# A two-layer decoder trunk on one core: one quarter's output product made plain, weight combinations made in other stages, operand sums in small steps, the last attention block by block

## The chip, the cores and the metric

The kernel runs on one core of one Trainium2 chip, in one launch. The metric is device time in microseconds; of several runs the median counts. Engines are named as the profile names them: PE multiplies matrices (PEld is its loading of weights), DVE, ACT and POOL work on vectors, SP issues nearly all transfers, in the order of its queue.

## What is computed

Sequence 2048, width 1024, float32. A first layer (A) gates with mixed values, a second (B) attends in three groups of 8 query heads over one shared set of keys and values.

```
# layer A
h = rms_norm(x, norm_g) * (1 + scale) + shift
u, v, z = jnp.split(h @ w_in, 3, axis=-1)          # each 2048 wide
v = rms_norm(jax.nn.gelu(v), sgu_g)
mixed = jnp.einsum('gts,bcsge->bctge', w_causal, v) + b_s
y = gelu(u) * mixed * jax.nn.silu(z)
x = x + gate * (y @ w_out)                         # the output product
# layer B: k, v from x @ w_kv (6 heads of 128, three groups)
qz = h @ w_in                                      # 24 query heads of 128, and z
o_g = banded attention of group g (128 keys back, dilation 1, 4, 16)
o = softmax over groups of their log-sums, times o_g, summed
x = x + gate * ((o * silu(z)) @ w_out)
```

## The kernel before

**Products.** Each float32 operand is held as a high part and a low part. A product of a 128-wide strip is three matmuls of 128x512 (`mm3`, L282): high by high, high by low, low by high. Weights come as 256 KB loads `raw_*` and `split` (L253) makes the two parts: ACT copies the high part, DVE subtracts to get the low one. Some products are Strassen–Winograd products of 2x2 blocks, with 7 block products in place of 8 and sums of operands, weights and results around them.

**Stages.** The 2048 tokens are four quarters of 512, numbered Q = 0 to 3 here; the "quarter 2" of the change's name is Q = 1. Layer A runs in halves H = 0 and 1. `layer_in(H)` (L1127) makes v (H = 0 with `plain_v`, H = 1 with `dense_v` for the weight blocks 4 and 5), then u and z in `gate_block`s with the mixing. `layer_out(Q)` (L1215) is the output product, then `proj_B(Q)` (L1332) makes layer B's projections: `kv_block(2)`, `kv_block(1)`, `q_block(2)`, `kv_block(0)`, `q_block(1)`, `q_block(0)`, `z_block`. The order is H = 0, Q = 0, Q = 1, H = 1, Q = 2, Q = 3. `finish()` is the last stage: the weighted sum of the three attentions and layer B's output product (`pf`).

**Output product.** For Q = 0 it is plain (`dense`, 384 matmuls). For Q = 1 to 3 it is `dense_o` (L445, 7 products, 336 matmuls). Its weights are the seven combinations 11, 21, 22, t1 to t4 of w_out, which `combine_out` (L387) makes once: for each h (2) and k (4) it loads w_out into `co` tiles, keeps the split parts as `cs` tiles and stores them to `wtd`; four subtractions run on POOL (L415). `o_weights` (L439) loads them back in 512 KB pieces.

**Side work.** Work beside the main products stands in generators, the fillers. `tick()` in the main loops steps them; `rate` says how many steps a tick gives. What a step writes lands in the engines' and SP's queues between the main work's instructions, and those queues run in order. The fillers that the change moves are `combine_out` (beside Q = 0's output product, rate 3.0), `more_side_work` (`combine_weights((4, 5))`: the v weights' combinations of H = 1, POOL subtractions `cw` at L340 to L343 and stores to `wt`; and `presplit`: layer B's w_out split and stored to `wod`; beside Q = 1's output product, rate 1.0), and attention of earlier quarters (`attend_local`, `wide_attention`). `sums_h` makes the sums of h that are operands of the Strassen products, at once where it is called. Scheduling by the framework can shift instructions within an engine's queue, so the order of the queues is shown where it matters.

## Time and profile before

| | |
|---|---|
| median of 3 runs (lowest, highest) | 3053.54 us (3048.94, 3057.72) |
| profiled execution | 3048.26 us, its span 3046.2 us |
| PE busy, share of span | 2878.5 us, 94% |
| PEld | 2385.4 us, 78% |
| DVE, ACT, POOL | 71%, 55%, 24% |
| mean granted clock of PE | 0.98 |
| transfers | 765.92 MB, 251 GB/s |

Stages in the profiled execution, by their first and last matmuls: first v product to 242 us; u and z of H = 0 to 592; output of Q = 0 592 to 715 and its projections to 950; output of Q = 1 950 to 1053, projections to 1323; v of H = 1 1323 to 1489; u and z 1489 to 1962; output of Q = 2 1962 to 2052; projections to 2274; output of Q = 3 2274 to 2387; projections to 2724; the last stage to 3041. Matmuls are pipelined, so a busy PE can still be waiting inside a busy interval: the distance from one matmul to the next is a better measure than busy time.

### The profile page before, as it was taken

What the parts mean: (1) busy time and instruction counts of PE and PEld (TensorE: products, weight loads), DVE (VectorE), ACT (ScalarE), POOL (GpSimd) and SP (SyncE); (2) the same over time, 40 slices, a digit from 0 to 9 for tenths busy, and PEclk for the clock granted to TensorE, in tenths of its full rate; (3) what the DMA queues carried; (4) which work ended last, traced back from release to release, by engine and by line L of the source; (5) the groups of instructions that cost most, each with busy time, mean ns of one, the idle gap of its engine ahead of it and who ended that gap; (6) DMA issues with size and microseconds to landing.
All of it is one profiled execution on the core that took longest, in us unless ns stands there. A gap on an engine that the chain in (4) does not pass through costs nothing. (4 is left out here: it accounts for less than half of the span.)

```text
span 3046.2 us, 44925 instructions
## 1 busy us (share of the span) xinstructions
PE 2878.5 (94%) x14338; PEld 2385.4 (78%) x14338; DVE 2159.3 (71%) x4033; ACT 1670.3 (55%) x3411; POOL 735.1 (24%) x975
## 2 busy tenths in 40 slices
PE   8899999978999898989999999999999999999999
PEld 5678888866787676768888888878888778878897
DVE  5777778667785565774557887957776867879782
ACT  4544444435564345765676676636554558865551
POOL 1102540032432232500001242401423321122212
PEclk9999999989999999999999999999999999999999
DMA  8898997578889979785445445697789667796643
GB/s 301 281 316 287 318 320 253 204 291 296 276 261 348 378 261 317 258 293 169 153 150 170 157 147 159 229 378 225 253 298 325 204 222 248 256 337 228 205 164 121
DMA packets 390080, 765.92 MB, mean 251 GB/s; under 512 B 43242, under 2 KB 99788, under 8 KB 387924
## 3 DMA queue, kind: packets, MB, share of 16 engines
q1 hardware_dynamic: 389844, 763.06, 73.3%
q8 instruction: 113, 1.85, 0.3%
q14 instruction: 123, 1.01, 0.1%
HBM read 552.53 MB, written 210.38 MB: 250 GB/s over the span
## 5 line engine op out<-in xcount | busy, mean ns | idle before, releaser
L284 PE MATMUL pd_kv<-w_kv,hkh 128*128 128x512 f32 x672 | 215.4, 400 | 13.0 <-DVE w_kv L256 9.0
L284 PE MATMUL pd_v<-w_v,opa 128*128 128x512 f32 x672 | 164.8, 402 | 12.7 <-ACT w_v L255 10.0
L284 PEld LDWEIGHTS pd_kv<-w_kv,hkh 128*128 128x128 f32 x672 | 127.7, 192 | 43.7 <-DVE w_kv L256 12.6
L284 PEld LDWEIGHTS pd_v<-w_v,opa 128*128 128x128 f32 x672 | 126.6, 192 | 43.4 <-ACT w_v L255 10.1
L284 PE MATMUL pd_kv<-w_kv,hkl 128*128 128x512 f32 x336 | 132.8, 396 | 0.0
L255 ACT ACTIVATE w_q<-raw_q 128x512 fp32r<-128x512 f32 x144 | 88.3, 627 | 62.2 <-DMA raw_q<-in_b_w_in_dram 30.1
L1555 ACT ACTIVATE pr<-pr,stat,rt 128x256 f32<-128x256 f32 (+1 forms) x192 | 104.1, 544 | 28.6 <-DVE stat L1549 24.2
L256 DVE TENSOR_TENSOR w_q<-raw_q,w_q 128x512 fp32r<-128x512 f32 x144 | 99.0, 707 | 28.6 <-ACT w_q L255 28.2
L1381 POOL TENSOR_SCALAR s_q<-s_q 128x4 f32<-128x4 f32 x96 | 24.0, 250 | 356.9 <-DVE s_q L1380 287.3
L1806 PE MATMUL pf<-wo,yb 128*128 128x512 f32 x256 | 106.0, 414 | 0.1
L1563 POOL TENSOR_TENSOR dg<-pr,ident 128x256 f32<-128x256 f32 x30 | 25.6, 854 | 321.8 <-ACT pr L1555 297.2
L284 PE MATMUL pd_o<-w_o,yh 128*128 128x512 f32 x256 | 85.4, 414 | 17.1 <-ACT w_o L255 14.6
L1808 PE MATMUL pf<-wo,yb 128*128 128x512 f32 x256 | 100.9, 394 | 0.5 <-DVE yb L1767 0.5
L1807 PE MATMUL pf<-wo,yb 128*128 128x512 f32 x256 | 100.5, 392 | 0.0
L1555 ACT ACTIVATE st_pr<-st_pr,stat,rt 128x256 f32<-128x256 f32 (+1 forms) x128 | 73.4, 575 | 31.2 <-DVE stat L1549 19.2
L1163 POOL TENSOR_SCALAR rvs<-rvs 128x8 f32<-128x8 f32 x2 | 0.8, 416 | 353.0 <-DVE rvs L1162 353.0
L1615 PEld LDWEIGHTS po<-kvr,pT 128*128 128x128 f32 x640 | 78.3, 191 | 9.8 <-ACT pT L1455 4.5
L1615 PE MATMUL po<-kvr,pT 128*128 128x128 f32 x640 | 81.6, 276 | 3.9 <-ACT pT L1455 2.4
L1814 POOL TENSOR_TENSOR of<-of,xr 128x512 f32<-128x512 f32 x32 | 41.4, 1293 | 176.2 <-DVE of L1813 153.3
L1180 ACT ACTIVATE vc<-vc,rvs 128x256 f32<-128x256 f32 x128 | 54.7, 498 | 53.2 <-DMA vc<-vd 42.8
L1545 DVE SCALAR_TENSOR_TENSOR pr<-dist,rt,ps 128x256 f32<-128x256 f32 (+1 forms) x192 | 70.8, 416 | 17.2 <-PE ps L1542 13.6
L340 POOL TENSOR_TENSOR cw<-cw 128x512 f32<-128x512 f32 x24 | 35.0, 1457 | 190.3 <-DMA cw<-in_a_w_in_dram 103.9
(1885 smaller groups left out, 8918.9 us busy)
## 6 DMA issues: line engine op xcount, KB each, us to landing
raw_q<-in_b_w_in_dram SPq DMA_DIRECT2D x144, 256.0 KB, 3.7
w_o<-wtd SPq DMA_DIRECT2D x72, 512.0 KB, 7.4
wtd<-cs SPq DMA_DIRECT2D x56, 512.0 KB, 3.5
qt<-qd SPq DMA_DIRECT2D x96, 260.0 KB, 3.2
wt<-cw SPq DMA_DIRECT2D x96, 256.0 KB, 4.2
od<-ot SPq DMA_DIRECT2D x96, 256.0 KB, 5.6
raw_kv<-in_w_kv_dram SPq DMA_DIRECT2D x84, 256.0 KB, 4.2
raw_v<-in_a_w_in_dram SPq DMA_DIRECT2D x80, 256.0 KB, 4.4
```

The source lines that it names most:

```text
L255: nc.scalar.activation(hi, src, AF.Copy)
L256: nc.vector.tensor_tensor(lo, src, hi.bitcast(F32), ALU.subtract)
L284: last_mm[0] = nc.tensor.matmul(pt, a, u[:, w, :], start=f, stop=e, skip_group_check=more)
L340: e.tensor_tensor(t1, t3, t1, ALU.subtract)
L1180: nc.scalar.activation(v[:, c, :], v[:, c, :], AF.Copy, scale=rvs[:, i:i + 1])
L1545: nc.vector.scalar_tensor_tensor(pr[:, i, :], dist[:, 256 - w:256], u["rt"][:, h:h + 1], psc[:, i, :], ALU.mult, ALU.add)
L1555: nc.scalar.activation(pr[:, i, :], pr[:, i, :], AF.Exp, bias=mneg[:, i:i + 1], scale=u["rt"][:, h:h + 1], accum_out=lsum[:, i:i + 1])
L1615: nc.tensor.matmul(po[:, h * P:(h + 1) * P], u["pT"][h // hp][:, h % hp, j, :], u["kv"][:, j, kh, 1, :], start=j == 0, stop=j == nk - 1)
L1806: nc.tensor.matmul(pt, yb[:, 0, k, :], w_[:, 0, :], start=k == 0, stop=False)
L1807: nc.tensor.matmul(pt, yb[:, 0, k, :], w_[:, 1, :], start=False, stop=False)
L1808: nc.tensor.matmul(pt, yb[:, 1, k, :], w_[:, 0, :], start=False, stop=k == KT - 1)
L1814: nc.gpsimd.tensor_tensor(o_, o_, xr, ALU.add)
```

## The change

- The output product of Q = 1 becomes plain: `fast = Q >= 2`.
- `combine_out` keeps only t1 to t4, its 32 subtractions run on DVE, and it stands beside Q = 1's projections (rates 2.4 and 0.8). The weights 11, 21 and 22 of Q = 2 and 3 are loaded raw and split each time.
- `more_side_work` stands beside Q = 0's projections (rates 2.6 and 1.1). The output products of Q = 0 and 1 have no side work (rate 0).
- `sums_h` is a filler whose steps load one k ahead; for H = 1 the sums are completed between products of `dense_v`.
- The gates of H = 1 run with rate 1.55 (1.7 before) and Q = 2's output with 2.0 (1.5).
- The last attention (`attend_local(3, ...)`): its group g = 1 starts beside Q = 3's z block, the local group follows block by block, each block weighed as it is done; no bursts, rate 6 (8).

```
-    wtd = dp.tile([2, 7, 4, P, 2, 512], F32, name="wtd")
+    wtd = dp.tile([2, 4, 4, P, 2, 512], F32, name="wtd")
...
-                yield from keep((4, t1), (5, t4))
-                yield from keep((6, t2))
                 for o, a, b in ((t1, t3, t1), (t3, t2, t3), (t2, t2, t1), (t4, t4, t2)):
-                    nc.gpsimd.tensor_tensor(o, a, b, ALU.subtract)
-                yield
+                    nc.vector.tensor_tensor(o, a, b, ALU.subtract)
...
     def o_weights(Q, w, h):
+        if w[0] != "t":
+            return wunits(a_w_out, 8 * h + 4 * (w[0] == "2"), 512 * (w[1] == "2"), f"o{Q}{w}{h}_", 4)
...
             for j in range(4):
-                if j == 2:
+                if j == 1:
                     ops.update({n: op_tile(f"a0{n}") for n in ("s1", "s2")})
-                    for _ in sums_h(0, ops, False):
-                        pass
+                    sa = sums_h(0, ops, False)
+                    fillers.append(sa)
+                    rate[0] = 2.2
                 plain_v(1, j, b)
+            complete(sa)
...
                 dense_v(1, b, ops, lambda t, n, src, dst, junk, b=b: v_put(1, t, 2 * (b - 4) + n, src, dst, junk),
-                        {} if b == 5 else {"11": lambda: sums(False, "s2", "s1"),
-                                           "21": lambda: sums(True, "s4", "s3", "22")})
+                        {} if b == 5 else {"11": lambda: complete(sa), "21": second,
+                                           "t1": lambda: complete(sb[0])})
...
-        rate[0] = 0.65 if H == 0 else 1.7
+        rate[0] = 0.65 if H == 0 else 1.55
...
-        fast = Q >= 1
+        fast = Q >= 2
...
-        rate[0] = 1.7 if Q < 3 else 3.4
+        if Q == 0:
+            fillers.append(more_side_work())
+        if Q == 1:
+            co.append(combine_out())
+            fillers.append(co[0])
+        rate[0] = (2.6, 2.4, 1.7, 3.4)[Q]
...
+        rate[0] = (1.1, 0.8, 0.0, 0.0)[Q]
         q_block(2)
...
-        def last(reached):
-            yield from near(NQ - 2, False, True)
-            yield from weights(NT - 2 * TPQ, NT - TPQ)
-            reached.append(1)
-            yield from attend_local(NQ - 1, False, True)
-            yield from weights(NT - TPQ, NT)
+        def last():
+            yield from far
+            for Q in (NQ - 2, NQ - 1):
+                todo = list(range(4 * Q, 4 * Q + 4))
+                for _ in near(Q, False, True):
+                    while todo and (0, todo[0]) in over:
+                        b = todo.pop(0)
+                        yield from weights(b, b + 1)
+                        weighed.add(b)
+                    yield
...
             drain()
-            fillers.append(combine_out())
-        if Q == 1:
-            fillers.append(more_side_work())
-        rate[0] = (3.0, 1.0, 1.5, 2.3)[Q]
+        rate[0] = (0.0, 0.0, 2.0, 2.3)[Q]
```

Four places in the queues. First SP's queue in the second half of Q = 0's output product, before: `raw_o` are weights of the product, `wtd<-cs` the stores of `combine_out`, `co` its loads.

```order
L263 DMA raw_o_0_3_5477<-in_a_w_out_dram 128x512
L410 DMA wtd<-cs_5324 128x1024
L410 DMA wtd<-cs_5341 128x1024
L410 DMA wtd<-cs_5344 128x1024
L410 DMA wtd<-cs_5385 128x1024
L410 DMA wtd<-cs_5388 128x1024
L410 DMA wtd<-cs_5399 128x1024
L410 DMA wtd<-cs_5431 128x1024
L410 DMA wtd<-cs_5434 128x1024
L263 DMA raw_o_0_4_5482<-in_a_w_out_dram 128x512
```

The same place in the changed kernel, and on into the first projection (`raw_kv`).

```order
L269 DMA raw_o_0_3_5371<-in_a_w_out_dram 128x512
L269 DMA raw_o_0_4_5376<-in_a_w_out_dram 128x512
L269 DMA raw_o_0_5_5381<-in_a_w_out_dram 128x512
L269 DMA raw_o_0_6_5386<-in_a_w_out_dram 128x512
L269 DMA raw_o_0_7_5391<-in_a_w_out_dram 128x512
...
L339 DMA cw_5931<-in_a_w_in_dram 128x1024
L269 DMA raw_kv_0_0_5957<-in_w_kv_dram 128x512
L269 DMA raw_kv_0_1_5962<-in_w_kv_dram 128x512
L355 DMA wt_0_127<-cw_5851 128x512
L355 DMA wt_1_128<-cw_5853 128x512
L355 DMA wt_2_129<-cw_5851 128x512
```

The eight stores between two weight loads are gone from the output product; stores of the v weights (`wt<-cw`) now stand between the weight loads of the projections.

On PE at the end of Q = 0's output product, before: `pt_b` are transposes of the normed rows, which the next projection's operands are made from; `pd_kv` is that projection.

```order
L284 MATMUL pd_o_3_5574<-w_o_1_7_5689,yh_5074 128x512 x2
L284 MATMUL pd_o_3_5574<-w_o_1_7_5689,yl_5075 128x512
L892 MATMUL pt_b_1_0_5811<-ident,xr_5084 128x128 x3
L892 MATMUL pt_b_1_2_5821<-ident,xr_5084 128x128 x3
L892 MATMUL pt_b_1_4_5831<-ident,xr_5084 128x128 x3
L892 MATMUL pt_b_1_6_5841<-ident,xr_5084 128x128 x3
L284 MATMUL pd_kv_0_5977<-w_kv_0_0_5937,hkh_5093 128x512 x2
```

The same place in the changed kernel.

```order
L290 MATMUL pd_o_2_5445<-w_o_1_5_5520,yh_5074 128x512 x2
L910 MATMUL pt_b_1_0_5621<-ident,xr_5084 128x128 x3
L910 MATMUL pt_b_1_2_5631<-ident,xr_5084 128x128 x3
L910 MATMUL pt_b_1_4_5641<-ident,xr_5084 128x128 x3
L910 MATMUL pt_b_1_6_5651<-ident,xr_5084 128x128 x3
L290 MATMUL pd_o_2_5445<-w_o_1_5_5520,yl_5075 128x512
L290 MATMUL pd_o_3_5446<-w_o_1_5_5520,yh_5074 128x512 x2
L290 MATMUL pd_o_3_5446<-w_o_1_5_5520,yl_5075 128x512
```

The transposes moved from behind the last matmul of the output product to a place with some 16 matmuls of that product still to come.

On DVE at the start of Q = 2's output product, in the changed kernel: `w_o` are the splits of the raw weights 11, 21 or 22, the other rows are attention (`stat`, `ot`, `pT`).

```order
L262 TENSOR_TENSOR w_o_0_17327<-raw_o_0_17328,w_o_0_17327 128x512
L1588 TENSOR_TENSOR stat_197<-stat_197,stat_198 128x2
L262 TENSOR_TENSOR w_o_1_17332<-raw_o_1_17333,w_o_1_17332 128x512
L262 TENSOR_TENSOR w_o_2_17337<-raw_o_2_17338,w_o_2_17337 128x512
L262 TENSOR_TENSOR w_o_3_17342<-raw_o_3_17343,w_o_3_17342 128x512
L1646 TENSOR_TENSOR stat_198<-stat_198 128x4
L1657 SCALAR_TENSOR_TENSOR ot_5_0_17371<-o_0_17242,stat_198,po_5_0_17362 128x128
L1647 TENSOR_TENSOR stat_197<-stat_197,stat_198 128x4
```

The kernel before has no such splits there: its weights of Q = 2 come split from `wtd`. PE's matmuls of the output product now wait for DVE's queue, which holds attention as well.

## Rows read from the trace of the kernel before

**Rows 1.** The page: the span and the busy time of PE and PEld.

```profile
PE 2878.5 (94%) x14338; PEld 2385.4 (78%) x14338; DVE 2159.3 (71%) x4033; ACT 1670.3 (55%) x3411; POOL 735.1 (24%) x975
```

**Rows 2.** Windows, undisturbed stretches: PE, PEld, DVE, ACT, POOL, clock, DMA share, GB/s.

```profile
835.80:950.40 114.60, 114.55 (x505) 94.55 (x504) 91.79 (x138) 70.94 (x117) 35.45 (x68) 1.00 0.83 272
291.40:314.00 22.60, 22.60 (x118) 19.28 (x116) 16.28 (x24) 9.23 (x16) 12.53 (x9) 1.00 0.92 326
314.00:333.10 19.10, 19.10 (x86) 15.75 (x86) 14.34 (x22) 9.76 (x19) 7.19 (x5) 1.00 0.99 335
```

**Rows 3.** Windows, the stages that the change touches, same columns.

```profile
100.00:242.00 142.00, 131.87 (x583) 107.08 (x582) 101.31 (x160) 58.66 (x121) 0.00 (x0) 0.95 0.89 309
592.10:714.80 122.70, 99.17 (x402) 79.01 (x400) 77.56 (x98) 49.97 (x88) 37.67 (x28) 0.88 0.82 305
714.80:814.00 99.20, 90.84 (x377) 71.59 (x377) 84.06 (x134) 62.88 (x122) 32.95 (x41) 0.94 0.77 266
950.40:1052.70 102.30, 84.61 (x354) 65.97 (x352) 43.77 (x62) 24.61 (x46) 28.35 (x24) 0.97 1.01 400
1052.70:1322.70 270.00, 243.71 (x1029) 193.17 (x1029) 187.78 (x293) 156.94 (x288) 93.85 (x142) 0.94 0.83 279
1322.70:1413.20 90.50, 80.95 (x351) 65.14 (x349) 60.84 (x101) 51.39 (x99) 0.00 (x0) 0.96 0.74 245
1962.40:2051.50 89.10, 83.45 (x390) 68.81 (x389) 55.10 (x89) 31.00 (x55) 10.43 (x14) 1.00 0.98 378
2273.60:2386.50 112.90, 110.45 (x618) 93.75 (x616) 82.67 (x159) 53.21 (x119) 39.97 (x58) 1.00 0.89 323
...
2724.40:3041.40 317.00, 307.57 (x1893) 268.11 (x1893) 227.53 (x626) 151.22 (x429) 76.99 (x45) 1.00 0.57 192
```

**Rows 4.** What PE waited for, 592 to 815 us: total us, times, longest.

```profile
PE pd_o L284 <- ACT w_o L255: 14.6, 3, 8.7
PE pt_b L892 <- DVE xr L1280: 6.4, 2, 6.3
PE pd_kv L284 <- DVE w_kv L256: 5.0, 1, 5.0
```

**Rows 5.** What SP's queue waited for, 592 to 770 us, same columns.

```profile
SPq L410 <- DVE cs L256: 57.1, 37, 5.8
```

**Rows 6.** Timeline of SP, then of PE, about 661 to 682 us: start, length, what.

```profile
661.22 10.32 SPq L410 DMA_DIRECT2D wtd<-cs  x7
...
674.08 2.13 SPq L263 DMA_DIRECT2D raw_o<-in_a_w_out_dram  x2
...
680.29 1.52 PE L284 MATMUL pd_o<-w_o,yh 128*128 128x512 f32 x2 [8.68 <-ACT w_o L255]
```

**Rows 7.** What PE waited for, 100 to 242 us.

```profile
PE pd_v L284 <- ACT w_v L255: 10.0, 2, 5.8
```

**Rows 8.** Timeline of ACT, then of PE, about 135 to 140 us.

```profile
135.66 2.32 ACT L255 ACTIVATE opa0s<-st_f0False 128x512 fp32r<-128x512 f32 x4
137.89 2.89 ACT L255 ACTIVATE w_v<-raw_v 128x512 fp32r<-128x512 f32 x5
...
138.56 1.65 PE L284 MATMUL pd_v<-w_v,opa 128*128 128x512 f32 x3 [4.17 <-ACT w_v L255]
```

**Rows 9.** What PE waited for, 1322 to 1490 us.

```profile
PE pd_v14a L284 <- DVE st_v14u L750: 7.3, 1, 7.3
```

**Rows 10.** Lines of the tiles `w_q` and `cw`: ns shortest/median/longest, first and last start.

```profile
L256 DVE TENSOR_TENSOR w_q<-raw_q,w_q x144: 676/685/1789, 766.3 to 2670.2; 128x512 fp32r<-128x512 f32 x144
...
L341 POOL TENSOR_TENSOR cw<-cw,cw x24: 1260/1294/1625, 261.5 to 1096.1; 128x512 f32<-128x512 f32 x24
```

**Rows 11.** The page, costliest groups: the mean of the score forms of attention on DVE.

```profile
L1545 DVE SCALAR_TENSOR_TENSOR pr<-dist,rt,ps 128x256 f32<-128x256 f32 (+1 forms) x192 | 70.8, 416 | 17.2 <-PE ps L1542 13.6
```

**Rows 12.** The page, DMA issues: how many, KB each, median us from issue to landing.

```profile
raw_q<-in_b_w_in_dram SPq DMA_DIRECT2D x144, 256.0 KB, 3.7
```

More of the change, by code (lines that the diff above doesn't have):

```diff
@@ L95, in tick, with complete @@
         fill(n)
+    def complete(g):
+        for _ in g:
+            pass
+        if g in fillers:
+            fillers.remove(g)
     def drain():
@@ L365, in trunk @@
     combined = set()
+    co = []
     flip = [False]
@@ L440, in o_weights @@
             u = wp.tile([P, 2, 512], F32R, tag="w", name=f"w_o{Q}{w}{h}_{k}")
-            last_ld[0] = nc.sync.dma_start(u.bitcast(F32), wtd[h, place[w], k])
+            last_ld[0] = nc.sync.dma_start(u.bitcast(F32), wtd[h, int(w[1]) - 1, k])
             us.append(u)
@@ L802, in make_h @@
         Q = 2 * H + half
-        xts = [load_x(Q * TPQ + t) for t in range(TPQ)]
+        if H:
+            xb = big.tile([P, TPQ, D], F32, tag="big", name=f"xa{Q}")
+            xts = [xb[:, t, :] for t in range(TPQ)]
+            for t in range(TPQ):
+                nc.sync.dma_start(xts[t], x[(Q * TPQ + t) * P:(Q * TPQ + t + 1) * P, :])
+        else:
+            xts = [load_x(Q * TPQ + t) for t in range(TPQ)]
         yield
@@ L856, in sums_h @@
         add = lambda o, a, b, op: nc.vector.tensor_tensor(o, a, b, op)
-        for k in range(4):
-            f = {}
-            for ns in (("11", "21"), ("12", "22")) if second else (("21", "22"), ("11",)):
-                load(ns, k)
+        fs = {}
+        for k in range(5):
+            if k < 4:
+                f = fs[k] = {}
+                for ns in (("11", "21"), ("12", "22")) if second else (("21", "22"), ("11",)):
+                    load(ns, k)
+            if k == 0:
+                yield
+                continue
+            k -= 1
+            f = fs.pop(k)
             if second:
@@ L1655, in put @@
                 outs.pop(0)()
+                n = len(over_of) and over_of.pop(0)
+                if n and n[2]:
+                    over.add(n[:2])
+        over_of = [u["id"] for u in us]
         load(0)
@@ L1750, in first @@
             ys[0] = prepare(0, ogs[0])
-        def last(reached):
-            yield from near(NQ - 2, False, True)
-            yield from weights(NT - 2 * TPQ, NT - TPQ)
-            reached.append(1)
-            yield from attend_local(NQ - 1, False, True)
-            yield from weights(NT - TPQ, NT)
+        weighed = set()
+        def last():
[7 more added lines that the diff above has]
+                        weighed.add(b)
+                    yield
+                for b in todo:
+                    yield from weights(b, b + 1)
+                    weighed.add(b)
         def make_yb(t):
@@ L1769, in finish @@
         fs = first()
-        fillers.append(fs)
-        rate[0] = 2.0
+        far = attend_local(NQ - 1, True, False, False)
+        fillers.extend((fs, far))
+        rate[0] = 4.0
         yield
-        drain()
-        reached = []
-        local = last(reached)
-        next(local)
-        fillers.append(local)
-        rate[0] = 8.0
+        complete(fs)
+        if far in fillers:
+            fillers.remove(far)
+        fillers.append(last())
+        rate[0] = 6.0
         ogs[1] = load(1)
@@ L1796, in finish @@
                         ys[t + 2] = prepare(t + 2, ogs[t + 2])
-                    if t + 3 == NT - TPQ:
-                        drain()
-                        ogs[t + 3] = load(t + 3)
-                    while t + 4 == NT - 2 * TPQ and not reached:
-                        fill(1)
-                    if t + 4 < NT and t + 4 != NT - TPQ:
-                        ogs[t + 4] = load(t + 4)
+                    for i in [t + 4] * (t + 4 < NT - 2 * TPQ) + [t + 3] * (NT - 2 * TPQ <= t + 3 < NT):
+                        while i >= NT - 2 * TPQ and i not in weighed:
+                            fill(1)
+                        ogs[i] = load(i)
                 for k in range(KT):
@@ L1842, in near @@
         yield from attend([(0, b) for b in range(4 * Q, 4 * Q + 4)], wrap, 3, 1 + (wrap or alt), wrap or alt)
+    over = set()
     def next_h():
@@ L1878, in ahead @@
                 ops.update({n: op_tile(f"a1{n}") for n in ("11", "12")})
-                fillers.append(next_h())
-                rate[0] = 1.7
+                hgen.append(next_h())
+                fillers.append(hgen[0])
+                rate[0] = 2.4
             else:
```

31 lines of the change are left out of this document (20 added, 11 removed).

## The prediction

> **What bounds the kernel now.** The page comes first: PE is busy 94% of the span, PEld 78% [rows 1]. No other engine is near that, so the time is PE's work plus what PE loses, and the question is where it loses. For that I need a price of undisturbed work. The windows over three stretches without waits give it: 504 matmuls of 128x512 in 114.6 us, 0.2275 us each; and the stretch with 32 small ones more is 22.60 − 19.10 = 3.5 us longer, 0.109 us for a small one [rows 2]. Lost time of a stage is then its length minus 0.2275 for each matmul of 128x512 and 0.109 for each of the rest. The windows over the stages [rows 3] give:
>
> - first v product, 100 to 242: 522 matmuls and 61 small, 142.0 − 118.8 − 6.6 = 16.6 lost
> - output of Q = 0: 384 and 18, 122.7 − 87.4 − 2.0 = 33.3
> - its projections up to 814: 360 and 17, 99.2 − 81.9 − 1.9 = 15.4; behind that nothing [rows 2]
> - output of Q = 1: 336 and 18, 102.3 − 76.4 − 2.0 = 23.9
> - its projections: 960 and 69, 270.0 − 218.4 − 7.5 = 44.1
> - first block of v of H = 1: 336 and 15, 90.5 − 76.4 − 1.6 = 12.5
> - output of Q = 2: 336 and 54, 89.1 − 76.4 − 5.9 = 6.8; of Q = 3: 336 and 282, 112.9 − 76.4 − 30.7 = 5.8
>
> Some 158 us, and the reader should see that the losses lie where the fillers write transfers and splits beside a product, not where attention runs.
>
> Which wait ends last there? In the output of Q = 0 PE waits for a weight's split, `w_o`, up to 8.7 us at once [rows 4]. The timeline names the source: SP sits on seven stores `wtd<-cs` from 661.2 to 671.5, issues the next weights' loads only at 674.1, and PE starts again at 680.3 after 8.68 us of nothing [rows 6]. Those stores wait for DVE's splits of `cs`: SP stood 57.1 us over 37 stores, 1.54 us each [rows 5]. PE's busy time leaves 122.7 − 99.2 = 23.5 us idle; the other 10 are work at the lower clock level after each wait (granted 0.88 on the mean, against 1.00 in rows 2).
>
> In the first v product two waits are 10.0 of the 16.6 us: ACT works on four `opa0s` parts of the sums at once, and five weight splits stand behind them [rows 7, 8]. In v of H = 1, 7.3 of 12.5 us is one wait for DVE [rows 9], where the sums are made whole between two products.
>
> **The change part by part.**
>
> *Plain product in Q = 1*: 48 matmuls more, 48 × 0.2275 = **+10.9**.
>
> *Last attention*: the order shows 32 transposes fewer, 32 × 0.109 = −3.5. In the last stage PE is busy 307.6 of 317.0 us [rows 3], so 9.4 idle is the most that steadier side work can take away, and as much again the most that I let the higher rate beside the z block cost. I take −2, since the bursts go. Together **−5.5** (bounds −13 and +6).
>
> *Sums in small steps, first v product*: the two bursts of ACT go. The same splits remain, four loads ahead, so waits up to one split of about 0.6 us can stay; 16.6 becomes 4, **−13** (bounds −16 and −5, if only the longer wait goes).
>
> *Output of Q = 0 without `combine_out`*: none of the `wtd` stores stands between weight loads any more; DVE has only 32 weight splits, 0.685 each [rows 10], 22 us in 87 of PE's, and a load of 256 KB lands 3.7 us after its issue [rows 12], well inside the 22 us of 96 matmuls ahead of it. The transposes `pt_b` now stand before some 16 matmuls, so the 6.4 us wait for the normed rows [rows 4] has 3.6 us of cover, and the wait behind it, 5.0 us for the first `w_kv` split, loses its cause, since its load no longer stands behind stores. 33.3 becomes 4, **−29** (bounds −33 and −15: half stays if the three waits for `w_o` are the loads' own time at a DMA share of 0.82).
>
> *Q = 0's projections get `more_side_work`*: 32 stores `wt<-cw`, 16 `wod<-wos`, 32 POOL subtractions, 16 splits; they lose the rest of `combine_out`, whose stores ran on past the output product. The weights of the projection, `raw_kv`, queue behind `wt<-cw` now, and PE's `pd_kv` waits for them. At the queue's price of 1.54 us a store [rows 5] the 48 are 74 us of SP's time, in a stretch that lasts 230; for DVE I added up the changed order, each instruction with the duration that its form has in the trace: some 179 us beside 215 of PE. I leave 14 us lost instead of 15.4, **−1.4** (bounds −10 and +25).
>
> *Output of Q = 1 without side work, plain*: before, it moved 512 KB pieces and side loads at 400 GB/s and a DMA share of 1.01. Now 32 loads of 256 KB feed 384 matmuls. 23.9 becomes 8, of which some 4 are a gap at the start, since the first splits stand behind the last results of the z block: **−16** (bounds −22 and −4).
>
> *Q = 1's projections get `combine_out`*: 32 stores in place of the 48 of `more_side_work` and of the copies for it; 32 DVE subtractions more, 32 × 0.685 = 22 us on DVE, and 24 splits fewer. By the order DVE has 39.1 beside PE's 39.1 in `q_block(1)` and 44.5 beside 40.6 in `q_block(0)`, so little is gained there. 44.1 becomes 34, **−10** (bounds −22 and +15).
>
> *v of H = 1*: 12.5 becomes 5, **−7.5** (bounds −10 and +2).
>
> *Outputs of Q = 2 and 3*: each gets 24 splits, 24 × 0.685 = 16.4 us of DVE. In Q = 3 DVE then has 113 beside 115 of PE: 5.8 becomes 14, **+8** (0 and +16). In Q = 2 the slower rate in the gates leaves 16 more steps of attention to the output product as well, each some 2 us of DVE (four score forms at 0.416 [rows 11] and smaller ones). By the order DVE has 68 us beside PE's 41 in the first part, where the splits of the raw weights stand among attention. The 27 us excess is the upper bound, 0 the lower, since the gates get as much DVE time back; I take nearer the middle, **+12**.
>
> Sum: 10.9 − 5.5 − 13 − 29 − 1.4 − 16 − 10 − 7.5 + 8 + 12 = −51.5. The profiled execution took 3048.3 (span 3046.2), 5.2 under the median of 3053.5. So 3048.3 − 51.5 = 2996.8 on its own base and **3002 against the median**.
>
> **A rule against it.** In the rows the split `w_q` takes 0.685 us at the median and 1.789 at most, and POOL's subtraction with two inputs about 1.29 [rows 10]; few of the 144 splits are long. The Trainium skill, in "SBUF — State Buffer", section "Who interferes with whom", says that a DVE instruction with two SBUF inputs and a GpSimd instruction that reads SBUF share a port pair as an exclusive lock, the loser fully blocked. The longest row, 1.789, is about a split and most of a subtraction, which agrees. By the rule the sum moves toward rival 3, by the median row it stays.
>
> **The rivals.**
>
> 1. *The stall moves with the stores.* 80 stores now stand beside projections (48 and 32): 80 × 1.54 = 123 us of SP. In Q = 0's output 41 of the 57 us of such waits came out at PE (33.3 and half of the 15.4 behind them), 0.73; the forecast leaves 48 of 123, 0.39. For it: the same queue, and loads still behind stores. Against: 270 us of Q = 1's projections with 48 stores lost only 44. At 0.57 PE loses 70, +22: **3024**.
> 2. *The same, in full: slower.* If each store's wait reaches PE, 123 − 48 = +75: **3077**. It decides for slower from a share of (51.5 + 9 + 48)/123 = 0.88 on. Against it: no stretch of the trace passes on so much.
> 3. *POOL's subtractions hold DVE in Q = 0's projections.* If each of the 32 held one DVE instruction for its whole 1.29 us, DVE has 41 us more against a slack of 215 − 179 = 36, bunched where `kv_block(2)` has 26 beside 24. PE would lose about 25: **3027**. Against: the median of 0.685 [rows 10]; long ones are the exception. The port rule of the Trainium skill named above would make it so.
> 4. *It doesn't do what it says.* If the waits in both output products and the first v product are the loads' own time, their 58 us stay: **3060**. Against: [rows 6], where the loads are not yet issued.
> 5. *More is hidden*: Q = 2 and 3 lose nothing more, projections 7 less: 3002 − 27 = **2975**.
>
> **How the numbers follow.** Forecast 0.56, with a range of its own of 2985 to 3020; rival 1 0.16, rival 2 0.06, rival 3 0.08, rival 4 0.07, rival 5 0.07. From 2972 to 3046 the forecast and the rivals 1, 3 and 5 lie inside, less their tails: 0.8. A measurement here tells some 0.3%, 9 us, from no change: under 3044 is faster, over 3063 slower. Forecast, 1, 3 and 5 make 0.87, of which 0.04 are tails into no change; rival 4 lies half on either side of 3060, with 0.01 of rival 1 above. So faster 0.83, same 0.09, slower 0.08.
>
> **What would show it.** The output of Q = 0 should take about 93 us with no wait of PE over 3 us for `w_o`, that of Q = 1 about 98, the first v product no wait over 1 us for ACT. In the projections of Q = 0 look for SP standing on `wt<-cw` and for long DVE splits beside POOL's `cw`; in Q = 2's output for `w_o` splits late behind attention. The prediction is wrong if the projections lose over 80 us together, or if either output product still loses over 15.

## The result, and the profile after

The changed kernel takes 3068.87 us (median of 19 runs, 3056.87 to 3077.60) against 3051.64 us for the kernel before (19 runs): a ratio of **1.0047, 95% interval 1.0035 to 1.0060**, so slower by some 14 us where 3002 was forecast. Its profiled execution took 3061.96 us with a span of 3060.3, which is 14.1 longer than the span before and 6.9 under its own median.

The page's first part reads as before, PE again busy 94% of the span, with 16 matmuls more (14354).

The windows over the stages answer to [rows 3], columns as there:

```profile
100.00:246.20 146.20, 133.69 (x588) 107.69 (x586) 99.83 (x159) 60.58 (x127) 0.00 (x0) 0.95 0.87 297
590.00:679.00 89.00, 89.00 (x402) 73.66 (x402) 42.56 (x64) 29.84 (x54) 3.33 (x5) 1.00 0.49 158
679.00:781.40 102.40, 91.90 (x378) 73.33 (x376) 74.66 (x108) 51.21 (x98) 49.77 (x54) 0.92 0.70 235
781.40:823.60 42.20, 22.20 (x97) 17.75 (x95) 12.94 (x22) 12.26 (x19) 23.50 (x31) 0.82 0.87 296
823.60:864.40 40.80, 40.79 (x168) 33.32 (x169) 30.04 (x47) 25.13 (x44) 10.66 (x18) 0.94 0.89 306
864.40:969.10 104.70, 84.91 (x337) 64.26 (x335) 72.11 (x108) 55.71 (x96) 24.70 (x47) 0.93 0.91 312
969.10:1061.40 92.30, 92.29 (x400) 75.83 (x401) 43.67 (x71) 29.30 (x55) 2.41 (x4) 0.96 0.48 155
1061.40:1336.90 275.50, 242.76 (x1032) 191.34 (x1030) 210.20 (x340) 169.37 (x314) 82.95 (x130) 0.95 0.82 280
1336.90:1425.50 88.60, 80.03 (x349) 64.55 (x347) 60.10 (x100) 50.44 (x98) 0.00 (x0) 0.96 0.74 244
1946.70:2061.70 115.00, 103.46 (x537) 86.59 (x536) 103.04 (x205) 56.07 (x116) 46.48 (x46) 0.96 0.75 267
2284.30:2396.10 111.80, 110.71 (x617) 93.71 (x616) 95.43 (x181) 66.44 (x143) 43.11 (x58) 1.00 0.79 269
```

Lost time by the prediction's own rule (length minus 0.2275 for each 128x512 matmul and 0.109 for each of the rest), before, forecast and after:

| stage | before | forecast | after |
|---|---|---|---|
| first v product (of its 100 to 246 us) | 16.6 | 4 | 20.2 |
| output of Q = 0 | 33.3 | 4 | 0 |
| projections of Q = 0, all | 15.4 | 14 | 69.8 |
| output of Q = 1 | 23.9 | 8 | 3.0 |
| projections of Q = 1 | 44.1 | 34 | 49.3 |
| first block of v of H = 1 | 12.5 | 5 | 10.8 |
| output of Q = 2 | 6.8 | 19 | 16.7 |
| output of Q = 3 | 5.8 | 14 | 4.8 |

The 69.8 are 18.5 in the third row of the windows (360 matmuls: `kv_block(2)`, `kv_block(1)` and `q_block(2)`), 20.4 in the fourth (`kv_block(0)`), 2.6 in `q_block(1)` and 28.3 in `q_block(0)` with the z block. Of the 28.3, 7.0 are a wait for the first weights of Q = 1's output product, which the prediction counted in that product ("a gap at the start"); by its count the table's two rows would read 62.8 and 10.0. One wait is nearly all of the fourth row's loss. What PE waited for, 679 to 969 us, its first rows:

```profile
PE pd_q01b L290 <- ACT w_q L261: 20.0, 1, 20.0
PE pd_q00a L290 <- ACT w_q00t L261: 3.8, 1, 3.8
PE pd_kv L290 <- DVE w_kv L262: 3.6, 1, 3.6
```

PE ends `kv_block(0)` at 803.6 us, and SP's timeline says why the next weights are not there (start, length, what), with PE's next start as the last row:

```profile
795.21 5.17 SPq L339 DMA_DIRECT2D cw<-in_a_w_in_dram  x2
804.84 2.24 SPq L1377 DMA_DIRECT2D kvd<-hs_k  x4
807.13 1.46 SPq L1242 DMA_DIRECT2D y<-yd  x3
812.83 2.36 SPq L1377 DMA_DIRECT2D kvd<-hs_k  x4
815.24 0.97 SPq L1242 DMA_DIRECT2D y<-yd  x1
816.26 2.92 SPq L269 DMA_DIRECT2D raw_q<-in_b_w_in_dram  x4
...
823.61 8.34 PE L290 MATMUL pd_q01b<-w_q,hob 128*128 128x512 f32 x24 [19.98 <-ACT w_q L261]
```

The first weight load of `q_block(1)` stands behind eight stores of the keys that `kv_block(0)` itself makes. Those can only go when that block is done and normed, so PE runs dry between the two blocks. POOL's norm factors (`hr_k`) stand behind subtractions of `cw` as well, as five pieces of the chain of work in that stretch show:

```profile
805.39 1.26 POOL cw L346
809.41 1.26 POOL cw L349
811.04 1.01 POOL hr_k L256
813.45 0.70 DVE hs_k L1350
816.26 6.64 DMA raw_q<-in_b_w_in_dram
```

In the kernel before five loads of `q_block(1)` stood ahead of the first of these stores, and six more (not shown) between the first four and the last four:

```profile
821.91 1.83 SPq L263 DMA_DIRECT2D raw_q<-in_b_w_in_dram  x4
823.83 0.38 SPq L263 DMA_DIRECT2D raw_q01t<-wt  x1
827.99 2.24 SPq L1347 DMA_DIRECT2D kvd<-hs_k  x4
```

The order of the changed kernel's queue could be read before the run, and the prediction did not look at this place.

### The profile page after: what moved, and what is told of

Read it like the earlier page. It is cut to its first block, busy times and chain, and to the rows that moved or that the text cites. A ratio compares the mean times of both kernels' runs of the same rounds, so it can differ in the third digit from the quotient of the medians.

```text
span 3060.3 us, 45093 instructions
## 1 busy us (share of the span) xinstructions
PE 2888.5 (94%) x14354; PEld 2391.7 (78%) x14354; DVE 2196.8 (72%) x4173; ACT 1700.7 (56%) x3468; POOL 748.1 (24%) x1007
## 4 chain that ended last, share of the span: by engine, by line
PE 44%; DMA 11%; DVE 10%; ACT 5%; issue 4%; POOL 3%; SPq 1%; POOLq 0%; DVEq 0%; ACTq 0%
PE pd_kv L290 5%; PE pd_o L290 3%; PE po L1651 3%; DMA qt<-qd 1%; PE pd_v15b L290 1%; PE pd_v15a L290 1%; DMA og<-od 1%; PE pm L1218 1%; DMA raw_q<-in_b_w_in_dram 1%; PE pd_o3a L290 1%; PE pd_v14a L290 1%; PE pd_v14b L290 1%; PE pq L1541 1%; PE pd_q20a L290 1%; PE pd_q21b L290 1%
## 5 line engine op out<-in xcount | busy, mean ns | idle before, releaser
L290 PE MATMUL pd_kv<-w_kv,hkh 128*128 128x512 f32 x704 | 222.7, 397 | 4.9 <-DVE w_kv L262 4.6
L290 PE MATMUL pd_o<-w_o,yh 128*128 128x512 f32 x512 | 160.9, 395 | 7.0 <-ACT w_o L261 7.0
L261 ACT ACTIVATE w_o<-raw_o 128x512 fp32r<-128x512 f32 x112 | 70.2, 630 | 111.1 <-PE pd_o L290 57.9
L290 PEld LDWEIGHTS pd_o<-w_o,yh 128*128 128x128 f32 x512 | 97.5, 190 | 28.2 <-ACT w_o L261 7.4
L262 DVE TENSOR_TENSOR w_o<-raw_o,w_o 128x512 fp32r<-128x512 f32 x112 | 78.1, 711 | 57.6 <-ACT w_o L261 57.1
L1599 POOL TENSOR_TENSOR dg<-pr,ident 128x256 f32<-128x256 f32 x38 | 31.8, 836 | 357.5 <-ACT pr L1591 293.3
L255 POOL TENSOR_SCALAR r_b<-sq 128x1 f32<-128x1 f32 x16 | 7.7, 479 | 398.4 <-DVE sq L1305 398.0
L290 PE MATMUL pd_o<-w_o,yl 128*128 128x512 f32 x256 | 100.8, 394 | 0.0
L1651 PEld LDWEIGHTS po<-kvr,pT 128*128 128x128 f32 x640 | 79.1, 192 | 18.5 <-POOL pT L1626 7.6
L1651 PE MATMUL po<-kvr,pT 128*128 128x128 f32 x640 | 83.2, 278 | 10.8 <-POOL pT L1626 5.4
```

The source lines that it names most:

```text
L261: nc.scalar.activation(hi, src, AF.Copy)
L262: nc.vector.tensor_tensor(lo, src, hi.bitcast(F32), ALU.subtract)
L290: last_mm[0] = nc.tensor.matmul(pt, a, u[:, w, :], start=f, stop=e, skip_group_check=more)
L1599: nc.gpsimd.tensor_tensor(dg, prev, ident.unsqueeze(1).broadcast_to([P, hp, P]), ALU.mult)
L1651: nc.tensor.matmul(po[:, h * P:(h + 1) * P], u["pT"][h // hp][:, h % hp, j, :], u["kv"][:, j, kh, 1, :], start=j == 0, stop=j == nk - 1)
```

## The experiments

Each ratio is that of the run's kernel to the kernel before on the same chip; the changed kernel's is 1.0047. "Changed kernel" is the base of all but `e7`. Lost time is worked out by the rule above from each run's windows.

**Which part of the side work costs.** `e3` moves only `presplit`, `e2` leaves out only POOL's subtractions for blocks 4 and 5, `e10` puts them on DVE.

```
e3  beside Q = 0's projections: fillers.append(combine_weights((4, 5)))
    beside Q = 1's output:      fillers.append(presplit()), rate 1.2
e2  combine():  if todo[i][0] >= 4: return
e10 combine():  e = nc.vector if todo[i][0] >= 4 else nc.gpsimd
```

> The changed kernel, with only the split of layer B's output weights (16 splits and stores, 18 steps) moved back beside quarter 1's output product (rate 1.2). In the changed kernel q block 0 and the z block of quarter 0 lose 28 us (7.0 of them the wait for the first weights of the output product). If SP's stores of these splits hold the weight loads: these two lose 5 to 12, quarter 1's output product loses 4 to 8 more, total down by 8 to 18 us. If the loss there is only a late echo of the v-weight combinations before it: the two blocks stay over 22 us.

Measured: ratio 0.9990 (0.9980 to 1.0000), 17 us off the changed kernel. The windows over `q_block(0)` and the z block, and over Q = 1's output product:

```profile
866.30:942.40 76.10, 76.10 (x337) 63.03 (x336) 64.20 (x97) 50.03 (x83) 25.10 (x47) 1.00 0.84 268
942.40:1034.30 91.90, 89.69 (x402) 73.44 (x401) 46.78 (x77) 36.80 (x69) 4.37 (x4) 1.00 0.78 279
```

The two blocks lose nothing (28.3 before the move), the 7.0 us wait for the next product's weights goes with them, and the output product is as long as in the changed kernel (91.9 against 92.3). The same 16 splits and stores cost 28 us beside one product and nothing beside the other. SP's own waiting on these stores does not tell the two apart: it is longer where they cost nothing. First the changed kernel's row (679 to 969 us), then this run's (942 to 1034 us):

```profile
SPq L382 <- DVE wos L262: 16.8, 10, 4.4
SPq L382 <- DVE wos L262: 26.2, 12, 7.4
```

> The changed kernel, with POOL's 32 subtractions of the v weights' combinations (blocks 4 and 5) left out; their loads and stores stay. Theory 1 (POOL's queue): the 20 us wait of PE behind kv block 0 goes, and quarter 0's projections fall from 290 by 25 to 40 us. Theory 2 (the 32 stores in SP's queue themselves, 1.54 us each as in the prediction's first rival): they stay within 10 us of 290. Theory 3 (the port that POOL and DVE share): DVE's splits there were 4.3 + 2.2 us longer than the normal 0.69, so the projections fall by some 7 us.

Measured: ratio 0.9976 (0.9967 to 0.9985). The first two blocks lose 2.8 in place of 18.5; `kv_block(0)` still loses 15.6, with a 15.1 us wait of PE:

```profile
685.30:771.90 86.60, 84.44 (x377) 68.84 (x376) 62.18 (x107) 51.01 (x98) 16.74 (x30) 1.00 0.82 275
771.90:809.30 37.40, 22.30 (x97) 17.68 (x95) 13.24 (x22) 12.50 (x18) 11.57 (x23) 0.86 0.93 338
```

None of the three theories alone: the subtractions make 16 us of the first loss and 5 of the 20 us wait, not the rest. How they do it shows on DVE. Its busy time in the first two blocks and `q_block(2)` is 62.2 us for 107 instructions here and was 74.7 for 108 in the changed kernel. Two groups, changed kernel first:

```profile
L262 DVE TENSOR_TENSOR w_q02t<-raw_q02t,w_q02t 128x512 fp32r<-128x512 f32 x16 | 14.9, 958 | 6.7 <-ACT w_q02t L261 6.6
L1294 DVE TENSOR_TENSOR xr<-xr,xo 128x512 f32<-128x512 f32 x2 | 3.4, 1763 | 0.0
L262 DVE TENSOR_TENSOR w_q02t<-raw_q02t,w_q02t 128x512 fp32r<-128x512 f32 x16 | 10.7, 689 | 9.4 <-ACT w_q02t L261 9.4
L1296 DVE TENSOR_TENSOR xr<-xr,xo 128x512 f32<-128x512 f32 x2 | 1.3, 684 | 0.0
```

Reductions (`s_q`, 675 against 681 ns) and operations on a product's result (`hs_k<-pd_kv`, 425 against 424) kept their length. PE's waits for DVE's splits in that stretch, 3.6 us for `w_kv` and 3.3 for `w_q`, are gone as well. The run takes the subtractions out of POOL's queue too, where norm factors stand behind them, so how much of the 16 us each way makes is open.

> The changed kernel, with the 32 subtractions of the v weights' combinations on DVE in place of POOL, nothing else. Without them the first two kv blocks and q block 2 of quarter 0 lost 3.0 us instead of 18.7, and its projections took 272 instead of 290. If it was POOL (its queue, or the port it shares with DVE): these blocks lose under 8 and the projections take 272 to 280 us, total down by 10 to 18 us. If it was the work as such, DVE's 32 x 0.61 = 20 us take its place: projections 285 to 300, total within 8 us.

Measured: ratio 1.0031 (1.0016 to 1.0046), against 1.0047 hardly told apart. The first two blocks lose 13.5 in place of 18.5:

```profile
682.70:780.10 97.40, 88.24 (x378) 69.51 (x377) 78.03 (x133) 51.58 (x100) 17.72 (x30) 0.98 0.74 248
```

So the subtractions cost 11 us there on DVE, where they cost 16 on POOL, nearer to the second reading. That does not split the 16 into a part of POOL and a part of the step. DVE's own instructions are back at their length (`w_q02t` 683 ns), but 24 subtractions of some 0.69 us, 16 us in all, now stand in its queue in that stretch; the run puts one load on DVE in place of another.

**The order of SP's queue behind `kv_block(0)`.**

```
e6   (on e3)  rate[0] = 0.0 ahead of kv_block(0), 1.1 behind it, for Q == 0
e14  ev0():   held = Q in (0, NQ - 1)         # was Q == NQ - 1
```

> As the run with the split of layer B's output weights moved back to quarter 1's output product, and with the v-weight combinations' steps paused during kv block 0 of quarter 0 and taken up in q block 1. In SP's queue of this build two weight loads of q block 1 stand ahead of the first store of that block's keys and nine ahead of the last, in the changed kernel none. If the 20 us wait behind kv block 0 is that order (the loads behind the stores, and those behind the block's end): its loss falls from 21 to under 6 us, q block 1 loses up to 8 more, total 12 to 18 us under that run. If it is the combinations' work itself, which is only put off: q block 1 loses what kv block 0 saves, total within 5 us.

Measured: ratio 0.9968 (0.9956 to 0.9980), 0.9990 without the pause. `kv_block(0)`, then `q_block(1)`:

```profile
781.50:803.60 22.10, 22.10 (x98) 17.97 (x98) 12.06 (x20) 8.73 (x15) 9.93 (x19) 1.00 0.96 332
803.60:855.90 52.30, 42.89 (x169) 32.73 (x168) 29.15 (x46) 26.72 (x44) 24.14 (x34) 0.93 0.85 290
```

The wait is gone (0.3 lost), but `q_block(1)` loses 14.1 in place of 2.9. The total fell by 7 us, between the two readings; order and work moved together here, which left them mixed.

> The changed kernel, with one edit: the stores of kv block 0's keys in quarter 0 are held until the first weights of q block 1 have been issued (as the kernel does it in the last quarter). The side work stays where the changed kernel has it. In SP's queue of this build four weight loads of q block 1 stand ahead of all eight of these stores, in the changed kernel none. If the order of SP's queue makes the 20.0 us wait: kv block 0 loses 5 to 13 us instead of 20.4 (four loads are 48 matmuls, 11 us) and the total falls by 6 to 15 us. If POOL's queue or the side work itself makes it: kv block 0 still loses over 17, total within 4 us.

Measured: ratio 1.0042 (1.0025 to 1.0059), which the interval does not tell from 1.0047. `kv_block(0)` loses 7.7 in place of 20.4, `q_block(1)` 10.8 in place of 2.6:

```profile
781.40:810.90 29.50, 22.15 (x98) 17.77 (x96) 11.47 (x19) 10.02 (x17) 21.60 (x31) 0.96 0.90 321
810.90:859.90 49.00, 43.31 (x169) 33.76 (x170) 29.69 (x47) 26.33 (x44) 10.94 (x19) 0.89 0.90 305
```

The order makes 13 of the 20 us at that place, as expected, but 8 come back one block later, where the held stores now stand ahead of the next weights. The four loads that were moved ahead feed 24 matmuls, 5.5 us, not the 48 that the expectation counted. Over both blocks the new order is worth 4.5 us, not 13.

**Where and how densely the side work runs.** `e1` puts `more_side_work` beside the u and z blocks of H = 0, `e5` beside Q = 1's output product at rate 3.0, `e11` leaves it where the change put it at less than half the rate.

```
e1   side_work(): yield from more_side_work(); gates of H = 0: rate 1.35 (was 0.65)
e5   beside Q = 1's output: fillers.append(more_side_work()); rate 3.0
     both: rates of Q = 0's projections 1.7 and 0.0, nothing beside them
e11  Q = 0's projections 1.0 and 0.45 (were 2.6 and 1.1), Q = 1's output 1.0
```

> The changed kernel, but the v-weight combinations and the split of layer B's output weights (48 filler steps) run beside the u and z blocks of the first half (rate 1.35 in place of 0.65) instead of beside quarter 0's projections, where the rates become 1.7 and 0. In the changed kernel quarter 0's projections took 290.1 us, of which 70 are lost. Theory 1 (the combinations hold POOL, and with it the norm factors, k's stores and the weight loads behind them; presplit's stores hold SP): the projections fall to 225 to 235 us, the u and z blocks (343.8 us) gain at most 12, the total falls by 45 to 60 us. Theory 2 (the loss in the projections comes from elsewhere, the transposes moved or the plain product ahead): projections stay over 270 us and the total within 15 us of the changed kernel.

Measured: ratio 1.0112 (1.0098 to 1.0126), slower still. The projections take 220.6 us and lose nothing, as theory 1 had it, but the u and z blocks take 433.3 us in place of 343.8:

```profile
246.00:679.30 433.30, 372.22 (x1612) 302.75 (x1613) 277.44 (x408) 170.84 (x298) 133.00 (x98) 0.91 0.85 291
```

Here PE's longest waits are for `vc` (29.7 us over 6), and SP stands 42.4 us on `cw` loads whose tile still waits for a store. That run raised the rate of the older side work too, so the 89 us are not the moved work's alone.

> The changed kernel, with all of the side work (v-weight combinations and the split of layer B's output weights, 48 steps) moved from quarter 0's projections back to quarter 1's output product, at rate 3.0. Theory 1 (the side work as a whole costs what the stretch beside it cannot hide; the projections are the worst place): quarter 0's projections fall from 290.1 to about 221 us, as where nothing ran beside them; quarter 1's output product rises from 92.3 to between 105 and 125 us; total 40 to 55 us under the changed kernel, some 1.0% under the kernel before. Theory 2 (any stretch pays the same 70 us for it): the output product rises to 150 us or more and the total is within 15 us of the changed kernel.

Measured: ratio 0.9970 (0.9958 to 0.9982). Projections without loss, 220.7 us; the output product:

```profile
900.30:1030.40 130.10, 96.89 (x402) 77.28 (x400) 52.14 (x77) 39.52 (x74) 45.57 (x37) 0.87 0.90 318
```

It loses 40.7, where 3.0 were lost without the side work: more than theory 1 allowed, less than theory 2. The total is some 24 us under the changed kernel, between the two as well. The same steps cost 38 us here in place of 69.8.

> The changed kernel, with the side work in the place of the changed kernel (quarter 0's projections) but at rates 1.0 and 0.45 instead of 2.6 and 1.1; what is left of it runs on beside quarter 1's output product at 1.0. If the rate is what costs: projections 235 to 255 us instead of 290, quarter 1's output product within 4 us of 92, total 30 to 50 us under the changed kernel. If the projections are the wrong host at any rate: they stay over 270, total down by under 20 us.

Measured: ratio 0.9985 (0.9972 to 0.9998), 19 us off the changed kernel. Projections, Q = 1's output, and Q = 1's projections are

```profile
681.00:917.80 236.80, 227.56 (x978) 183.90 (x976) 170.59 (x264) 134.65 (x237) 100.94 (x142) 0.98 0.80 267
917.80:1015.60 97.80, 91.20 (x402) 74.79 (x401) 42.66 (x65) 31.82 (x59) 14.26 (x11) 0.97 0.63 213
1015.60:1312.80 297.20, 253.48 (x1017) 196.89 (x1016) 218.72 (x354) 173.87 (x324) 79.11 (x130) 0.91 0.84 291
```

53 us are gained in the first, 5.5 and 21.7 given back in the next two, where the left-over steps meet `combine_out`. The first stage is in the range of the first reading, the total in that of the second. Not all of the 53 is the rate's: none of the 16 splits of `presplit` ran in the projections here (5 ran beside the output product, 11 behind it), and `e3` had shown 28 us for those. The nearer comparison is `e3`, which has the combinations alone there at the old rates: its projections (680.9 to 942.4 us) lose 41 us, here 16.6 with 26 of the 32 subtractions. Yet the totals of the two runs, 0.9990 and 0.9985, are hardly told apart.

**The plain product alone.**

```
e7 (on the kernel before)  fast = Q >= 2     # was Q >= 1
```

> The kernel before, with one edit: quarter 1's output product plain, its side work as before beside it. 48 matmuls more are +10.9 us. In the kernel before that product took 102.2 us and lost 24.0. If that loss came from the product's seven weight combinations of 512 KB each at a DMA share of 1.01: it falls under 8 and the product takes 90 to 98 us, total 4 to 12 us under the kernel before. If it came from the side work beside it: the loss stays at 18 to 26, the product takes 107 to 116, total 5 to 14 us over the kernel before.

Measured: ratio **0.9927** (0.9913 to 0.9940). The output product takes 90.6 us with the side work beside it at rate 1.0 and loses 1.5:

```profile
949.60:1040.20 90.60, 89.28 (x401) 73.48 (x400) 39.35 (x58) 28.17 (x53) 31.64 (x26) 1.00 0.79 273
```

One line of the change, with 48 matmuls more, is 22 us faster, more than either reading had. 11.7 us of it are this product; the projections behind it are 8.6 shorter (261.4 in place of 270.0), which was not taken apart. In the kernel before PE waited in this product for the stored combinations themselves, 14.6 us in all:

```profile
PE pd_o1b L284 <- DMA w_o1t<-wtd: 6.5, 3, 2.7
PE pd_o1a L284 <- DMA w_o<-wtd: 4.4, 4, 3.4
PE pd_o1a L284 <- DMA w_o1t<-wtd: 3.7, 3, 1.9
```

So the loss of 23.9 went with those 512 KB loads (400 GB/s in [rows 3], 273 here), and the side work did not have to move for it. Whether moving the side work alone would have done it too is not shown: no run has the old product without it. Nor does the 1.5 here stand for all of the side work, as `e9`'s expectation takes it: 22 of the 32 subtractions and none of the 16 splits of `presplit` ran beside this product, in `e5` all.

**The operand sums and the last attention.**

```
e4   sums_h of H = 0 at once, as in the kernel before
e12  if j == 0: (was 1) ... fillers.append(sa)      # and no rate[0] = 2.2
e8   finish() and its attention as in the kernel before
```

> The changed kernel, with the operand sums of the first half made at once, as in the kernel before. The first v product took 227.2 us in small steps, 223.0 in the kernel before. If the small steps cost there: about 223, total down by 3 to 5 us, with two waits of PE for ACT of 4 to 6 us. If both forms cost the same and 4 us are scatter: within 2 us of the changed kernel.

Measured: ratio 1.0057 (1.0041 to 1.0074), no difference from 1.0047. The stage took 224.7 us, which its own scatter between profiles (224.5 to 229.6 where this part was the change's) does not tell from 227.2.

> The changed kernel, with the first set of operand sums begun one block earlier and without the higher rate (1.6 in place of 2.2). In the changed kernel's SP queue 12 and 15 loads of the sums' inputs stand in one row ahead of the v weights' loads; here 9, 3 and 11. If the two waits of PE in the first v product (5.0 and 6.2 us) are those rows of loads: the first is under 3 us, the stage takes 221 to 225 us instead of 227.2. If they are ACT's splits of the sums: both waits go. If neither: 226 to 229.

Measured: ratio 0.9996 (0.9982 to 1.0011), some 16 us off the changed kernel. The first v product:

```profile
18.60:225.00 206.40, 201.34 (x861) 150.51 (x862) 137.57 (x225) 105.53 (x218) 16.41 (x21) 0.99 0.89 300
```

Both waits for `w_v` are gone, as the second reading (ACT) had it, but 227.2 becomes 206.4, which is less than any of the three allowed; some 6 of it come back in the u and z blocks (350.3 in place of 343.8). The edit did two things, an earlier start and a lower rate for everything beside the product; which of them did it was not taken apart, so it does not decide between SP's rows and ACT's splits.

> The changed kernel, with the last attention as in the kernel before (bursts, rate 2.0 and 8.0, 32 transposes more). The z block of quarter 3 and the last stage took 361.3 us before and 363.3 to 372 us in the profiles since. If the block-by-block form costs: 358 to 362 us, total 2 to 8 us under the changed kernel. If it saves, as the prediction had it (5.5 us): total 3 to 8 us over.

Measured: ratio 1.0050 (1.0035 to 1.0065). The z block and the last stage took 367.9 us against 363.3: no difference that the times show, so neither reading holds.

**The parts together.** `e9` spreads all side work at low rates; `e13` is `e9` with `e12`'s edit.

```
e9   rates: Q = 0's output 1.0 (combine_out beside it), its projections 0.8;
     Q = 1's output 1.0 (more_side_work beside it), its projections 1.7,
     also for the fillers added behind Q = 1's output (was 2.4)
```

> The changed kernel, with its side work spread at a low rate: the combinations of the output weights (40 steps) beside quarter 0's output product at rate 1.0 (3.0 in the kernel before, 0 in the changed one) and on into its projections at 0.8; the v weights' combinations and the split of layer B's output weights beside quarter 1's output product at 1.0 and on into its projections at 1.7. If it is the number of side steps per matmul that costs (48 steps cost 41 us beside an output product at rate 3.0, 1.5 us at rate 1.0): quarter 0's output product loses under 8, its projections under 20, quarter 1's output product under 4, its projections 30 to 40, total 2990 to 3015 us, the fastest of all. If each step costs the same wherever it stands: the 34 us of quarter 0's output product come back and the total is 3025 to 3045 us.

Measured: ratio **0.9891** (0.9869 to 0.9914), 3017.69 us. Q = 0's output, its projections, Q = 1's output:

```profile
592.60:681.50 88.90, 88.90 (x401) 73.62 (x400) 52.33 (x81) 35.21 (x64) 2.41 (x4) 1.00 0.68 237
681.50:915.20 233.70, 222.96 (x977) 182.47 (x976) 186.41 (x303) 145.61 (x259) 70.60 (x116) 0.99 0.84 279
915.20:1012.30 97.10, 92.03 (x401) 75.26 (x400) 43.68 (x64) 30.34 (x57) 31.89 (x26) 0.96 0.78 267
```

Beside Q = 0's output product `combine_out`, in its smaller form at rate 1.0, costs nothing; in the kernel before that product lost 33 us beside it. Three things differ between the two: the rate, the number of splits that run there (12 of 32 here, 42 of 56 before), and the engine of the subtractions (DVE here, POOL before, where DVE's splits of `cs` took 911 ns on the mean, here 692). The rest runs on beside the projections, which lose 13.5. Q = 1's output loses 8, where under 4 were expected, and the total is 3 us over the expected range. The reading that each step costs the same wherever it stands (3025 to 3045) is out. `e7`'s one line alone had made 22 of these 33 us.

> The run with the side work spread at a low rate, and with the first set of operand sums begun one block earlier at the lower rate, as in the two runs before. If the two gains are separate (36 us against the kernel before by the one, some 15 us against the changed kernel by the other, each in its own stage): first v product 205 to 209 us as there, quarter 0's output product still without loss, total 10 to 18 us under the run with the side work spread alone, 2998 to 3010. If the sums only took the place of work that then comes late in the u and z blocks: the total is within 5 us of that run.

Measured: ratio **0.9824** (0.9803 to 0.9845), 2998.78 us: the fastest of all, 1.8% under the kernel before. The first stage takes 206.7 us and Q = 0's output 89.1; the two gains add up.

## Why the prediction was wrong, point by point

- **Output of Q = 0: right.** 33.3 became 0 (forecast 4), all that was there to gain.
- **Output of Q = 1: right.** 23.9 became 3.0, or 10.0 with the gap at its start that the prediction counted here (forecast 8, 4 of them that gap). `e7` shows that the plain product alone does this, with side work still beside it. The prediction had shared the gain between the two.
- **Projections of Q = 0: the step that failed.** "I leave 14 us lost instead of 15.4, −1.4 (bounds −10 and +25)": measured 69.8, +54. It priced 48 stores at 1.54 us, 74 in all, and let most of them hide, because a DVE sum of 179 beside 215 of PE looked like room. The price was misread: [rows 5] gives the mean of 37 waits of SP on `cs`, not the cost of a store. In the changed kernel SP waited some 26 us on the 48 stores (7.7 on `wt<-cw`, 18.0 on `wod<-wos`), not 74. The DVE sum was right without POOL's subtractions (177.1 us in `e2`), but with them the same instructions took 189.7. And the sum over the whole stretch hid where the work falls. Three things show in place of the step: `presplit` beside `q_block(0)` and the z block 28 us (`e3`), POOL's subtractions in the first two blocks and `q_block(2)` 16 (`e2`), and the 20 us wait behind `kv_block(0)`, 13 of it by the order of SP's queue (`e14`), though 8 of those return a block later.
- **Why this host is worse.** The rows of the two places without `presplit` point to it: in `q_block(0)` and the z block (`e3`) DVE is busy 64 of 76 us at a DMA share of 0.84; in Q = 1's plain output product (changed kernel) 44 of 92 at 0.48. There each weight tile feeds four row tiles, in the q and z blocks two, so these need twice the loads and splits per matmul. That the same `presplit` is free in the one and 28 us in the other is shown; that this is the reason is argued.
- **The rate was no term of this step.** The changed rates 2.6 and 1.1 stand in no sum; the prediction speaks of a rate only for the gates of H = 1 and for the z block before the last stage. With them lowered in the same place (`e11`) the loss falls from 69.8 to 16.6, but `presplit` had then left the place, and 27 us come back in the two stages that the rest of the work spills to. A lower rate in one stage is fewer steps in that stage, and what rate alone is worth was not taken apart.
- **Rival 2 (3077) was nearest in size**, at a chance of 0.06, and that is luck. Stores and loads in one queue are part of the truth, but its mechanism, 1.54 us of each store reaching PE, is not what the rows show (26 us of waits on the 48 stores in the projections of Q = 0), and leaving subtractions out (`e2`) freed 18 us with every store in place. Rival 1's share, 41 of 57, is 0.72 and not 0.73; by it its 3024 comes to some 3022.
- **Rival 3, POOL against DVE, had more in it than its chance of 0.08.** It allowed 25 us. Leaving the subtractions out (`e2`) shortens the projections of Q = 0 by 18 and takes 12.6 us off DVE's busy time there. The median of `w_q`, the argument against it, looked at a split that the subtractions hardly touch: it keeps 685 ns in the changed kernel too, while 16 `w_q02t` rise to 958 and two `xr` to 1763. The Trainium skill ("SBUF — State Buffer", section "Who interferes with whom") says that a DVE instruction with two SBUF inputs contends with a GpSimd instruction that reads SBUF. GpSimd is POOL here, and the trace agrees: 689 ns became 958 for such a split, and the reductions, with one input, kept their length. What is not separated is POOL's queue, which holds the norm factors, and which `e2` empties as well.
- **First v product: failed.** 16.6 became 20.2, not 4. The step took ACT's burst for the cause. In the changed kernel the sums go in small steps and two waits of 5.0 and 6.2 us stay: 12 and 15 loads of the sums' inputs still stand in a row in SP's queue ahead of the weights, and ahead of the first wait SP also stood 5.1 us on a store of the gate. At the first wait ACT is idle until the weight's load lands; at the second, splits of the sums still stand ahead of the weights' in ACT's queue. With the sums begun earlier and less beside the product (`e12`) both go.
- **v of H = 1: failed.** 12.5 became 10.8, not 5: the wait of 7.3 us for DVE became one of 4.0 for DVE and one of 2.9 for ACT.
- **Projections of Q = 1: failed**, 49.3 instead of 34, near the upper bound. `combine_out` there was taken for cheaper than what it replaced. Without it, with the rest of `more_side_work` there and at other rates (`e9`), they take 262.7 us in place of 275.5; which of the two it was is open.
- **Outputs of Q = 2 and 3:** 16.7 against a forecast of 19, and 4.8 against 14: Q = 3's DVE at 95 of 112 us still hid its splits. What moved to Q = 2's output (25.9 us longer) had left the u and z blocks of H = 1 (28.0 shorter), so this pair cost nothing.
- **Last attention:** −5.5 forecast, +2.0 in the profile, nothing that the times show (`e8`).
- **Its own signs.** The prediction called itself wrong if the projections lose over 80 us together: they lose 119. Long DVE splits beside POOL's `cw`, which it said to look for, came; SP standing on `wt<-cw` hardly did (7.7 us).

In sum: the two output products lose 54 us less (45 were forecast), and the projections of Q = 0 lose 54 us more. What was left is the 10.9 us of the 48 matmuls and some 3 us of all other terms together, among them 5 us more lost in Q = 1's projections.

## What to carry to other kernels

Side work has no price of its own: the same 16 splits and stores cost 28 us beside one product and nothing beside another, and a wait in a queue's row is not the price of a store. So ask of a move where the loads and splits per matmul are fewest, before adding up an engine's busy time over a long stretch. Thin spreading (`e9`) gave the fastest kernels here, though rate, number of steps and place moved together in it. Look for DVE instructions that get longer beside POOL's: compare the same groups with and without them, not one group's median. And read in the queue's order whether the next block's first weight load stands ahead of the stores that wait for this block's end.

## What the runs showed of the hardware

After the 20 us wait PE worked at its lower level at first: 24 matmuls took 8.34 us, where 24 at 0.2275 are 5.5. The granted clock of those 8.3 us was 0.68, and in the 8 us behind them 1.00:

```profile
823.61:831.90 8.29, 8.29 (x25) 6.40 (x26) 4.07 (x6) 3.70 (x6) 0.00 (x0) 0.68 0.93 339
```

After a wait of 3.56 us, at 943 us, 24 matmuls took 8.25. So these two waits, of very different length, each cost some 2.8 us beyond their own; one of 3.82 us, at 890 us, cost 1.9 (7.32 us for 24), and one of 1.28 us, at 899 us, 0.7 (6.15).

On DVE, operations with two inputs from SBUF got longer while POOL's subtractions ran (689 to 958 ns for 16 splits, 684 to 1763 for two of `xr`), and went back when the subtractions were left out (`e2`) or put on DVE (`e10`).
